# Padding three small tiles so that float32r matmul operands start on multiples of 256 bytes, with a new list of the mixer's steps, in a two-layer decoder trunk

## The chip, the cores and the metric

The kernel runs on one core of one Trainium2 chip. The metric is the device time of one execution in microseconds. A profiled execution has a time of its own and, inside it, a span from the first to the last instruction; the positions in every profile row are counted from the start of that span.

TensorE is called PE in the profile (its weight loads PEld), VectorE DVE, ScalarE ACT, GpSimd POOL, and SyncE, which issues all transfers, SP.

## The reference

A trunk of two layers on 512 tokens of width 1024. Layer 0 mixes tokens with causal average pooling over four windows, layer 1 with stick-breaking attention over 16 heads of 64. Each is followed by a squared-ReLU MLP of width 4096, and both have RMSNorms before and after.

```python
def pool_mixer(h, w_grp, scale):          # four groups of 256 channels, windows 2, 4, 8, 16
    for g, w in enumerate(POOL_WINDOWS):
        outs.append((upper - lower) / count - hf[:, :, sl])      # windowed mean minus identity
    y = jnp.einsum('bsgc,gcd->bsgd', y, w_grp)
    return y * scale

def stick_breaking_attention(q, k, v):    # per block of 128 queries
    z = q_blk @ k_blk.T / 8
    log1m = jnp.where(mask, -jax.nn.softplus(z), 0.0)
    excl = lax.cumsum(log1m, axis=3, reverse=True) - log1m
    a = jnp.where(mask, jnp.exp(jax.nn.log_sigmoid(z) + excl), 0.0)
    return a @ v_blk

def sq_relu_mlp(h, w_up, w_down):
    return jnp.square(jax.nn.relu(h @ w_up)) @ w_down

for layer in range(2):
    h = rms_norm(x, mix_pre_g[layer])
    m = pool_mixer(h, ...) if layer == 0 else stick_breaking_attention(h @ w_q, k, v) @ w_o
    x = x + rms_norm(m, mix_post_g[layer])
    h = rms_norm(x, mlp_pre_g[layer])
    x = x + rms_norm(sq_relu_mlp(h, w_up[layer], w_down[layer]), mlp_post_g[layer])
    if layer == 0:
        k, v = split(rms_norm(x, kv_norm_g) @ w_kv)
```

## The kernel before

**Three products for one.** Nearly every matmul is float32r, a 4-byte format that keeps fewer bits than float32. To keep the precision, an operand is split into a high part (a cast on ACT, L246 or L132) and a low part (the difference on DVE, L247 or L134), and a product becomes three matmuls: high by high, high by low, low by high. The helpers are `mm3` (L267 to L269), `up_block` (L607 to L609) and `Seven.product` (L497). Each matmul loads a stationary operand of 128 columns and streams a moving operand of up to 512.

**The stages.** The tokens are four tiles of 128 rows, x0 to x3.

1. The mixer (layer 0's pooling) from the start to some 49 us. It multiplies each tile by a band matrix (L708), then by the group weights (L731), normalizes, transposes (L765) and splits the result into `xnh` and `xnl`, the high and low parts of the normalized, transposed residual stream, eight slices of 512 tokens each.
2. The first MLP. `up_block` makes one of 32 blocks of 128 hidden channels: 8 slices, three matmuls each, with an up weight stationary and `xnh` or `xnl` moving. The down projection takes 28 of the 32 blocks in five groups by a scheme with seven products in place of eight (class `Seven`; `a` is the stationary operand, `w` the moving one) and the last four plainly through `contract`, with the squares `sq` stationary and the down weights `dn` moving. Blocks of up and products of the group before alternate on PE. The first four up blocks of each MLP are run in two halves of 256 tokens.
3. Attention. Values come from `mm3` with `xnh` or `xnl` stationary and 256 columns moving; keys and queries from `up_block`. Scores are L915 and L916 (q stationary, k or its low part kl moving), the running product is a scan on DVE (L929), the weights are transposed (L947), and L957 multiplies them (ah, al moving) with the values (v stationary). The output projection goes through `contract` with `ohl` stationary and the output weights moving; the last two of its eight weights stand in the tiles that held `v` and `w` (named w and h, l in the profile).
4. The second MLP, as the first. The kernel ends with the last update's norm and stores.

**What sets the order.** Past the mixer the order comes from a scheduler that knows the program order and each instruction's estimated cost, with hints (`issue_after`, `manual_schedule`). In the mixer the order on PE, ACT, DVE and POOL is that of the list `MIX_ORDER` (L42): each word is a step, a letter and its arguments, and each engine runs its steps in the order of the list. The letters used below, with tile t and half h: `q` squares of x (ACT, L679), `r` the power -1/2 (POOL, L690), `b` the band matrix scaled (DVE, L698), `P` pooling (PE, L708), `c` its copy from PSUM to `yt` (ACT, L723 or L719), `L` group weights scaled, four pieces for each of two weight tiles (DVE, L667), `M` group weights (PE, L731), `s` squares of the mixed result (ACT, L250), `g` its gain (DVE, L739), `e` and `E` their total and power, `A` the residual added (DVE, L749), `w` and `v` squares and power for the next norm, `N` that norm (DVE, L756), `T`, `H`, `X` transposes, high and low part (L765, L773, L777), `h`, `l` high and low part of one of the first four up weights (L785, L789), `U` the first half of an up block (PE, L607 to L609). "Tile" 4 stands for the 90 border rows at the seams between tiles, which are loaded into `edge` on their own. A weight's `h` also issues its load on SP (L782) into one of two `raw` buffers, and the third and fourth loads wait until an `l` has freed one.

**Where tiles lie.** A pool lays its tiles one behind another in each partition of SBUF, in steps of 32 bytes. The pool `keep` begins at byte 384: four x tiles of 4104 bytes (4128 with padding), `ident` (512), `gc` (96), `mhalf` (4, takes 32), then `xnh` and `xnl` (16384 each) and the small `stat` tiles; the pools `work` and `wts` follow, and then one pool for the current stage. In the attention pool two tiles `u0` and `u1` of 5124 bytes lie ahead of `v`, `k`, `q`, `w`, `ah`, `al` and `ohl`.

Of the kernel before, what the change touches and what calls it, by code (L numbers as in the profile page):

```python
# [10 lines left out]
F32 = mybir.dt.float32  # L11
# [4 lines left out]
P = 128  # L16
D = 1024
S = 512
T = S // P
KC = D // P  # L20
# [10 lines left out]
EPS = 1e-6  # L31
# [5 lines left out]
NSEG = 1280  # L37
# [3 lines left out]

MIX_ORDER = [  # L42
    (w[0], [int(c) for c in w[1:]])
    for w in """z8 S0 q0 C0 S1 r0 b0 z1 P00 L00 L02 C1 c00 P01 L03 q4 L01 L13 r4 L10 L11 c01 L12 M00 M01 b4 q1 r1 b1 s00
    q2 s01 g00 e0 r2 P40 c40 g01 E0 b2 A0 P10 q3 c10 P11 r3 w0 P20 b3 v0 c11 M10 N00 P30 N01 h0 M11 T00 P31
    l0 s10 h1 c30 g10 s11 l1 c20 e1 g11 H00 E1 A1 X00 c31 h2 T01 M30 M31 w1 v1 l2 s30 N10 s31 M20 H01 N11 T10
    g31 P21 X01 H10 T11 c21 H11 M21 s21 X10 X11 e3 s20 g30 E3 U0 A3 w3 g21 e2 g20 h3 E2 A2 w2 v3 U1 N30 N31
    v2 l3 N21 T30 H30 U2 T21 T31 H31 N20 H21 T20 X30 X31 H20 X21 X20 U3""".split()
]


# [18 lines left out]
def trunk(ctx, tc, x, consts, gcol, grow, pw, wup, wdn, wq, wk, wv, wo, out):  # L70
    nc = tc.nc
    pool = lambda name, bufs=1, **kw: ctx.enter_context(tc.tile_pool(name=name, bufs=bufs, **kw))
    keep = pool("keep")
# [9 lines left out]
    def name(s):  # L83
        uid[0] += 1
        return f"{s}{uid[0]}"
# [4 lines left out]

    xt = [keep.tile([P, D + 2], F32, tag=f"x{t}", name=f"x{t}") for t in range(T)]
    ident = keep.tile([P, P], F32, tag="ident", name="ident")
    gc = keep.tile([P, 3 * KC], F32, tag="gc", name="gc")
    for n in NS:
        nc.sync.dma_start(xt[0][:, n], x[TS[0], n])
    mhalf = keep.tile([P, 1], F32, tag="mhalf", name="mhalf")
# [308 lines left out]
    class Seven:  # L405
# [32 lines left out]
        def squares(self):  # L438
            self.r = self.mp.tile([P, 2, MOST, S], F32, tag="r", bufs=2, name=name("r"))
# [172 lines left out]
    with tc.tile_pool(name="mix0", bufs=1, reuse_waits="tile") as mp:  # L612
# [7 lines left out]
        edge = mp.tile([3 * EDGE, D + 2], F32, tag="edge", name="edge")  # L620
        windows = {**dict(enumerate(xt)), T: edge}
        for w in windows.values():
            nc.vector.memset(w[:, D:], (EPS * D) ** 0.5)

        BANDS = (P, REST, BORDER)
        starts = [0, 4 * P, 4 * (P + REST)]
# [22 lines left out]
        sts, band, pys, pms, ms, xns, pts, pus = {}, {}, {}, {}, {}, {}, {}, {}  # L649
# [27 lines left out]
        def mean_square(t, col):  # L677
            r = rows(t)
            nc.scalar.activation(  # L679
                junk[r, : D + 1], windows[t][:, : D + 1], ACT.Square, scale=D**-0.5,  # L680
                accum_out=sts[t][r, col : col + 1],
            )

        def squares(t):
            sts[t] = keep.tile([P, 8], F32, tag=f"stat{t}", bufs=4, name=name("stat"))
            mean_square(t, 0)

        def power(t, col):
# [102 lines left out]
        def half_up(j):  # L791
            pus[j] = ps(), get(("up", 0, j))
            up_block(*pus[j], slice(0, S // 2))

        steps = {
            "q": squares, "r": lambda t: power(t, 0), "b": scaled_band, "P": pooled, "c": pooled_out,
            "S": spread, "C": spread_out, "L": linear, "M": mixed, "s": mixed_square, "g": mixed_gain,
            "e": total, "E": lambda t: power(t, 4), "A": added, "w": lambda t: mean_square(t, 6),
# [14 lines left out]
    with tc.tile_pool(name="att", bufs=1, reuse_waits="tile") as ap:  # L813
# [75 lines left out]

        begin = ap.tile([P, NSEG], mybir.dt.bfloat16, tag="begin", name="begin")  # L890
        nc.gpsimd.memset(begin, 0.0)
        us = [ap.tile([P, NSEG + 1], F32, tag=f"u{a}", name=f"u{a}") for a in range(2)]
        for lo, n in SEG.values():
            c = min(n - P, 1)
            d = begin[:, lo + n - P - c : lo + n]
# [178 lines left out]
```

## Time and profile before

| What | Value |
|---|---|
| median of 3 runs | 972.52 us (972.29 to 977.75) |
| the profiled execution: its time | 971.85 us |
| its span | 970.0 us |
| granted TensorE clock over the span | 0.997 |
| busy PE, PEld | 951.6 us, 801.0 us |
| busy DVE, ACT, POOL | 709.8 us, 568.7 us, 144.2 us |
| read from and written to HBM | 122.68 MB, 33.55 MB |

A group's row gives line, engine, operation, tiles and shapes, the count, then busy time and mean duration of one in ns, then the engine's idle time just before it and what ended that. A matmul's duration runs from its start to the modelled arrival of its last result, so that durations of successive matmuls overlap: 512 columns take 390 to 395 ns each, though the next one starts sooner. How fast PE goes is read from the distance between starts. A timeline row gives the start, the duration, engine, line, operation and count of a run of like instructions, and in brackets the idle time before it with the releaser. A row of windows gives a stretch of the span, its length, and each engine's busy time with the count of instructions that reach into it.

### The profile page before, as it was taken

How to read it: one execution, taken by the hardware profiler on the slowest of the kernel's cores; microseconds unless marked ns; L12 is line 12 of the kernel's file. 1: busy time of each engine (PE TensorE's matmuls, PEld its weight loads, DVE VectorE, ACT ScalarE, POOL GpSimd, SP SyncE). 2: the span in 40 equal slices, each digit the busy share in tenths (PEclk: the TensorE clock that was granted, in tenths of full speed). 3: DMA queues.
4: the chain of work that ended last, by engine and by line, in shares of the span. 5: the costliest groups of instructions: out<-in, count | busy, mean ns of one | idle time of the engine just before them, and what ended most of it. 6: DMA issues, size and time to landing. Idle time of an engine off the chain costs nothing.

```text
span 970.0 us, 12402 instructions
## 1 busy us (share of the span) xinstructions
PE 951.6 (98%) x4761; PEld 801.0 (83%) x4761; DVE 709.8 (73%) x736; ACT 568.7 (59%) x974; POOL 144.2 (15%) x108
## 2 busy tenths in 40 slices
PE   8999999999999999999999999989999999999997
PEld 6998888888888889888788887888888888888885
DVE  4856797988969966576477787855596876857856
ACT  6657889788865636455655563555544444443632
POOL 2120310502204014000000000301130300403103
PEclk9999999999999999999999999999999999999999
DMA  7544879697696840521624243332503233132012
GB/s 260 187 140 147 309 265 372 228 330 278 232 333 262 304 151 2 217 88 44 244 104 174 88 153 109 131 111 85 191 26 134 105 123 117 44 130 109 29 37 87
DMA packets 43683, 157.03 MB, mean 162 GB/s; under 512 B 4494, under 2 KB 4878, under 8 KB 43625
## 3 DMA queue, kind: packets, MB, share of 16 engines
q1 hardware_dynamic: 43625, 156.25, 45.0%
q8 instruction: 37, 0.61, 0.2%
q14 instruction: 21, 0.17, 0.1%
HBM read 122.68 MB, written 33.55 MB: 161 GB/s over the span
## 4 chain that ended last, share of the span: by engine, by line
PE 92%; DVE 3%; ACT 2%; issue 1%; DMA 1%; SPq 0%; POOL 0%; DVEq 0%; POOLq 0%; ACTq 0%
PE ps L497 28%; PE ps L609 15%; PE ps L607 15%; PE ps L608 15%; PE ps L268 4%; PE ps L269 4%; PE ps L267 4%; PE ps L957 2%; PE ps L947 1%; PE ps L731 1%; DVE e L929 1%; PE ps L915 1%; PE ps L916 1%; DMA edge<-in_x 1%; PE ps L708 1%
## 5 line engine op out<-in xcount | busy, mean ns | idle before, releaser
L497 PE MATMUL ps<-w,a 128*128 128x512 f32 x1176 | 278.8, 390 | 0.0
L608 PE MATMUL ps<-xnl,w 128*128 128x512 f32 (+1 forms) x712 | 265.0, 372 | 0.1
L609 PE MATMUL ps<-xnh,w 128*128 128x512 f32 (+1 forms) x712 | 265.1, 373 | 0.0
L607 PE MATMUL ps<-xnh,w 128*128 128x512 f32 (+1 forms) x712 | 265.0, 373 | 0.0
L497 PEld LDWEIGHTS ps<-w,a 128*128 128x128 f32 x1176 | 220.9, 188 | 47.4
L608 PEld LDWEIGHTS ps<-xnl,w 128*128 128x128 f32 x712 | 134.3, 189 | 25.2 <-DVE xnl L247 0.3
L609 PEld LDWEIGHTS ps<-xnh,w 128*128 128x128 f32 x712 | 134.1, 188 | 25.4
L607 PEld LDWEIGHTS ps<-xnh,w 128*128 128x128 f32 x712 | 134.0, 189 | 24.4
L134 DVE TENSOR_TENSOR w<-raw,w 128x1024 fp32r<-128x1024 f32 x62 | 82.2, 1328 | 62.7 <-ACT w L132 62.7
L132 ACT CAST w<-raw 128x1024 fp32r<-128x1024 f32 x62 | 65.0, 1049 | 87.8 <-PE ps L609 83.4
L506 DVE TENSOR_TENSOR y<-ps,y 128x512 f32<-128x512 f32 x124 | 83.4, 684 | 39.7 <-PE ps L497 39.7
L246 ACT CAST a<-r 128x768 fp32r<-128x768 f32 (+1 forms) x60 | 47.5, 792 | 70.5 <-PE ps L497 46.8
L452 POOL TENSOR_TENSOR s<-r 128x768 f32<-128x768 f32 (+1 forms) x10 | 20.5, 2048 | 382.0 <-ACT r L530 382.0
L247 DVE TENSOR_TENSOR a<-r,a 128x768 fp32r<-128x768 f32 (+1 forms) x60 | 60.1, 1004 | 18.5 <-ACT a L246 18.4
L246 ACT CAST w<-e 128x1536 fp32r<-128x1536 f32 (+1 forms) x30 | 42.0, 1398 | 44.5 <-DVE e L471 33.2
L292 POOL TENSOR_TENSOR y<-y,grow 128x512 f32<-128x512 f32 x12 | 18.7, 1556 | 316.4 <-ACT xn L250 316.4
L452 POOL TENSOR_TENSOR r<-r 128x768 f32<-128x768 f32 (+1 forms) x20 | 52.2, 2608 | 59.3 <-DVE a L247 58.5
L247 DVE TENSOR_TENSOR w<-e,w 128x1536 fp32r<-128x1536 f32 (+1 forms) x30 | 55.9, 1862 | 3.1 <-ACT w L246 2.7
L929 DVE TENSOR_TENSOR_SCAN e<-u,begin 128x1280 f32<-128x1280 f32 x16 | 45.1, 2822 | 13.3 <-ACT u L923 13.0
L143 ACT ACTIVATE apart<-apart,gc 128x128 f32<-128x128 f32 (+1 forms) x132 | 43.0, 405 | 0.0
L250 ACT ACTIVATE xn<-y 128x512 f32<-128x512 f32 (+1 forms) x25 | 15.4, 615 | 41.8 <-DVE y L359 41.8
L247 DVE TENSOR_TENSOR w<-xn,w 128x1536 fp32r<-128x1536 f32 (+1 forms) x20 | 33.0, 1651 | 6.4 <-ACT w L246 6.4
(137 smaller groups left out, 1486.5 us busy)
## 6 DMA issues: line engine op xcount, KB each, us to landing
raw<-in_wup SPq DMA_DIRECT2D x62, 512.0 KB, 4.1
w<-kept SPq DMA_DIRECT2D x58, 512.0 KB, 4.1
kept<-wx SPq DMA_DIRECT2D x30, 512.0 KB, 4.3
w<-in_wdn SPq DMA_DIRECT2D x8, 1536.0 KB, 6.7
kept<-apart SPq DMA_DIRECT2D x24, 512.0 KB, 3.6
xn<-in_wdn SPq DMA_DIRECT2D x8, 1536.0 KB, 8.0
raw<-in_wdn SPq DMA_DIRECT2D x8, 512.0 KB, 3.7
apart<-in_wk SPq DMA_DIRECT2D x7, 512.0 KB, 6.5
```

The lines of the kernel that those rows point to most:

```text
L132: nc.scalar.copy(hi, raw)
L134: nc.vector.tensor_tensor(out=lo, in0=raw, in1=hi.bitcast(F32), op=ALU.subtract)
L143: nc.scalar.mul(c, c, gc[:, lo + k : lo + k + 1])
L246: latest["act"] = nc.scalar.copy(hi, src)
L247: latest["dve"] = nc.vector.tensor_tensor(out=lo, in0=src, in1=hi.bitcast(F32), op=ALU.subtract)
L452: sub = lambda out, x, y, op=ALU.subtract: nc.gpsimd.tensor_tensor(out=out, in0=x, in1=y, op=op)
L497: nc.tensor.matmul(bank, a[:, x, q, TS[t]], w[:, z, q], start=start and q == 0 and k == 0, stop=q == self.n - 1 and k == 2, skip_group_che ...
L506: nc.vector.tensor_tensor(out=part, in0=bank, in1=part, op=ALU.add)
L607: nc.tensor.matmul(pu[:, cols], wh[:, k, :], xnh[:, k, cols], start=k == 0, stop=False)
L608: nc.tensor.matmul(pu[:, cols], wh[:, k, :], xnl[:, k, cols], start=False, stop=False)
L609: nc.tensor.matmul(pu[:, cols], wl[:, k, :], xnh[:, k, cols], start=False, stop=k == KC - 1)
L929: nc.vector.tensor_tensor_scan(out=e[:, ::-1], data0=u[:, 1:][:, ::-1], data1=begin[:, ::-1], initial=0.0, op0=ALU.mult, op1=ALU.max,)
```

## The change

Four edits change where tiles lie. `gc` gets 32 more elements (128 bytes) of which nothing is used; the `stat` tile of the border rows has 16 elements instead of 8; `u1` gets 55 more elements, unused. The two extra columns of the x tiles are now addressed as two, which is what they were. The list of the mixer's steps is another one; it has the same steps.

```diff
-    for w in """z8 S0 q0 C0 S1 r0 b0 z1 P00 L00 L02 C1 c00 P01 L03 q4 L01 L13 r4 L10 L11 c01 L12 M00 M01 b4 q1 r1 b1 s00
...
+    for w in """z8 q0 S0 r0 C0 b0 S1 z1 P00 L01 C1 L02 L00 P01 L03 L12 c00 c01 M00 q4 L10 r4 L11 s00 L13 b4 q1 r1 M01 s01
...
-    gc = keep.tile([P, 3 * KC], F32, tag="gc", name="gc")
+    gc = keep.tile([P, 3 * KC + 32], F32, tag="gc", name="gc")[:, : 3 * KC]
...
-            nc.vector.memset(w[:, D:], (EPS * D) ** 0.5)
+            nc.vector.memset(w[:, D : D + 2], (EPS * D) ** 0.5)
...
-            sts[t] = keep.tile([P, 8], F32, tag=f"stat{t}", bufs=4, name=name("stat"))
+            sts[t] = keep.tile([P, 16 if t == T else 8], F32, tag=f"stat{t}", bufs=4, name=name("stat"))
...
-        us = [ap.tile([P, NSEG + 1], F32, tag=f"u{a}", name=f"u{a}") for a in range(2)]
+        us = [ap.tile([P, NSEG + 1 + 55 * a], F32, tag=f"u{a}", name=f"u{a}")[:, : NSEG + 1] for a in range(2)]
```

In the two built programs the operands of the float32r matmuls begin so many bytes past a multiple of 256 (the count is that of matmuls in the program):

| Matmuls | count | moving operand, before -> after | stationary operand, before -> after |
|---|---|---|---|
| up and projections, 512 columns (L607 to L609) | 1704 | 128 -> 0 | 0 -> 0 |
| up and projections, 256 columns (L607 to L609) | 432 | 128 -> 0 | 0 -> 0 |
| values (L267 to L269, 256 columns) | 384 | 0 -> 0 | 128 -> 0 |
| output projection (L267 to L269, ohl) | 192 | 0 or 64 -> 0 | 64 -> 0 |
| scores (L915, L916) | 128 | 64 (k), 0 (kl) -> 0 | 64 -> 0 |
| attention weights by values (L957) | 128 | 64 -> 0 | 64 -> 0 |
| seven products (L497) | 1176 | 0 -> 0 | 0 -> 0 |
| plain down products (L267 to L269, dn and sq) | 204 | 0 -> 0 | 0 -> 0 |

`xnh` begins at byte 17536 before (68 x 256 + 128) and 17664 after (69 x 256); `k` of the first head at 162112 (633 x 256 + 64) and 162560 (635 x 256). The pools behind `keep` begin 256 bytes later.

The new list moves instructions on four engines inside the mixer. On ACT, its steps after the first square of x0 and the first copy of the scale row stood so before (a copy `scale`, then tile 0's pooled halves into `yt`, and the squares of x, of the border rows `edge` and of mixed results into `stat`):

```order
L723 COPY yt<-ps_143 128x4x128
L679 ACTIVATE junk,stat_158<-edge 90x1025
L723 COPY yt<-ps_152 128x4x128
L679 ACTIVATE junk,stat_179<-x_71 128x1025
L250 ACTIVATE junk,stat_134<-ps_167 128x512
L679 ACTIVATE junk,stat_185<-x_72 128x1025
```

and stand so now:

```order
L723 COPY yt<-ps_143 128x4x128
L723 COPY yt<-ps_152 128x4x128
L679 ACTIVATE junk,stat_166<-edge 90x1025
L250 ACTIVATE junk,stat_132<-ps_161 128x512
L679 ACTIVATE junk,stat_175<-x_71 128x1025
L250 ACTIVATE junk,stat_132<-ps_178 128x512
L679 ACTIVATE junk,stat_206<-x_72 128x1025
```

The second copy into `yt` (step c01) has moved ahead of the border rows' squares (q4), and the squares of tile 0's first mixed half (s00) ahead of those of x1 (q1).

On PE the same list stands, from tile 0's second mixed half on, before (`pw` are the group weights, `band` the scaled band matrices, `xn` the normalized rows):

```order
L731 MATMUL ps_172<-pw_100,yt 128x256 x4
L708 MATMUL ps_192<-band_177,edge 128x46 x8
L708 MATMUL ps_209<-band_182,x_71 128x114 x4
L708 MATMUL ps_217<-band_182,x_71 128x114 x4
L708 MATMUL ps_224<-band_206,x_72 128x114 x4
L731 MATMUL ps_233<-pw_99,yt 128x256 x4
L708 MATMUL ps_239<-band_229,x_73 128x114 x4
L731 MATMUL ps_249<-pw_100,yt 128x256 x4
```

and now:

```order
L731 MATMUL ps_178<-pw_100,yt 128x256 x4
L708 MATMUL ps_185<-band_173,edge 128x46 x8
L708 MATMUL ps_196<-band_194,x_71 128x114 x4
L708 MATMUL ps_201<-band_194,x_71 128x114 x4
L708 MATMUL ps_223<-band_218,x_72 128x114 x4
L731 MATMUL ps_231<-pw_100,yt 128x256 x4
L731 MATMUL ps_237<-pw_99,yt 128x256 x4
L708 MATMUL ps_245<-band_229,x_73 128x114 x4
```

The first five stand in the same places; of what follows, tile 1's second half is multiplied ahead of the first. Past the mixer each engine has at most a few neighbours exchanged: on SP the second weight load of the first MLP has moved ahead of one of a later key weight.

More of the change, by code (lines that the diff above doesn't have):

```diff
@@ L43 @@
     (w[0], [int(c) for c in w[1:]])
-    for w in """z8 S0 q0 C0 S1 r0 b0 z1 P00 L00 L02 C1 c00 P01 L03 q4 L01 L13 r4 L10 L11 c01 L12 M00 M01 b4 q1 r1 b1 s00
[L45 to L48, printed above, removed]
+    for w in """z8 q0 S0 r0 C0 b0 S1 z1 P00 L01 C1 L02 L00 P01 L03 L12 c00 c01 M00 q4 L10 r4 L11 s00 L13 b4 q1 r1 M01 s01
+    e0 P40 b1 P11 P10 q2 c40 r2 c11 E0 q3 g00 b2 g01 r3 c10 P21 A0 b3 M11 w0 M10 s11 c21 v0 P31 N00 g11 s10
+    T00 P30 h0 M21 e1 c31 g10 E1 c30 N01 A1 P20 H00 T01 w1 X00 h1 v1 l0 s21 N11 M30 T11 c20 N10 T10 H01 M20
+    l1 H11 X11 H10 X10 s30 M31 X01 h2 s20 h3 g21 l2 s31 g20 e2 g30 E2 e3 E3 U0 A2 w2 g31 U1 A3 v2 U2 l3 N20
+    w3 T20 H20 v3 N31 T31 N30 N21 T30 H31 X20 X31 T21 H30 X30 U3 H21 X21""".split()
 ]
```

## The prediction

> **What bounds the kernel now.** I read the page's engine totals and its chain of waits first, then busy time by stage.
>
> ```profile
> PE 951.6 (98%) x4761; PEld 801.0 (83%) x4761; DVE 709.8 (73%) x736; ACT 568.7 (59%) x974; POOL 144.2 (15%) x108
> ...
> PE 92%; DVE 3%; ACT 2%; issue 1%; DMA 1%; SPq 0%; POOL 0%; DVEq 0%; POOLq 0%; ACTq 0%
> ...
> 49.00:366.00 317.00, 317.00 (x1425) 260.71 (x1424) 258.45 (x232) 231.64 (x384) 57.58 (x26) 1.00 0.71 256
> 390.00:630.00 240.00, 236.70 (x1381) 207.66 (x1380) 170.22 (x200) 131.99 (x292) 10.02 (x11) 1.00 0.37 136
> 637.00:900.00 263.00, 263.00 (x1198) 216.77 (x1198) 183.07 (x158) 127.07 (x153) 44.99 (x19) 1.00 0.30 106
> ```
>
> The last three rows are stretches of the span (length, then PE, PEld, DVE, ACT, POOL busy, granted clock, DMA share): the first MLP, attention, the second MLP. PE is 92% of the chain, and in both MLPs it is busy for the whole stretch while the next engine, DVE, works 258.45 of 317.00 and 183.07 of 263.00. So the time is how far apart matmuls start, plus the few waits that the mixer and attention leave. A busy PE hides the first of these; the starts in the timeline show it. First the groups by form, for the counts:
>
> ```profile
> L497 PE MATMUL ps<-w,a 128*128 128x512 f32 x1176 | 278.8, 390 | 0.0
> L609 PE MATMUL ps<-xnh,w 128*128 128x512 f32 x568 | 224.5, 395 | 0.0
> L608 PE MATMUL ps<-xnl,w 128*128 128x512 f32 x568 | 224.2, 395 | 0.0
> ...
> L268 PE MATMUL ps<-w,ohl 128*128 128x512 f32 x56 | 22.4, 399 | 2.2 <-DVE w L134 2.2
> ...
> L267 PE MATMUL ps<-h,ohl 128*128 128x512 f32 x8 | 3.2, 395 | 0.0
> ```
>
> Then a stretch near the end of the second MLP (start, duration; only PE's rows are kept), and two windows asked for PE alone:
>
> ```profile
> 922.95 0.40 PE L607 MATMUL ps<-xnh,w 128*128 128x512 f32 x1
> ...
> 928.54 8.34 PE L497 MATMUL ps<-w,a 128*128 128x512 f32 x36
> 936.72 0.39 PE L267 MATMUL ps<-dn,sq 128*128 128x512 f32 x1
> ...
> 944.88:959.83 14.95, 14.95 (x67) 1.00 0.19 70
> 505.87:517.02 11.15, 11.15 (x50) 1.00 0.26 94
> ```
>
> From 922.95 to 928.54 stand one up block's 24 matmuls (8 slices, L607 to L609): 5.59/24 = **232.9 ns** apart. From 928.54 to 936.72 stand 36 of L497: 8.18/36 = **227.2 ns**. The first window holds 66 of the down projection's plain products (L267 to L269, dn and sq; the 67th reaches in from ahead): 14.95/66 = 226.5 ns. The second holds the 48 of a key and a query projection (two more reach in): 11.15/48 = 232.3 ns. All are 512 columns of float32r behind a 128-column weight load, without a wait, at clock 1.00. By the change's table of addresses the two at 227 have both operands on a multiple of 256 bytes; up and the projections have the moving one (xnh, xnl) 128 bytes past it.
>
> **The change part by part.**
>
> *Up blocks and projections.* 568 triples of 512 columns start 128 bytes off before and 0 after. 448 of them are in the MLPs (28 blocks of 8 in each; the other 4 blocks go in halves), 120 in attention. At L497's 227.2: 1344 x (232.9 - 227.2) = 7.7 us, and 360 x (232.3 - 227.2) = 1.8 us. **Together -9.5 us**, all on the path, since nothing else holds PE in these stretches; the padding adds no instruction. Bounds: 0, if the address isn't the cause; with the best row (226.5) 1344 x 6.4 + 360 x 5.8 = -10.7.
>
> *Output projection and attention products.* Here the stationary operand (ohl) or both (k and q) lie 64 bytes off:
>
> ```profile
> 604.86 0.39 PE L269 MATMUL ps<-h,ohl 128*128 128x512 f32 x1
> ...
> 607.41 0.39 PE L268 MATMUL ps<-l,ohl 128*128 128x512 f32 x1
> ...
> 571.61 0.39 PE L915 MATMUL ps<-k,q 128*128 128x512 f32 x1
> ...
> 572.07 0.33 PE L915 MATMUL ps<-k,q 128*128 128x384 f32 x1
> ```
>
> Eleven starts with ohl from 604.86 to 607.41: 231.8 ns. Against 227.2 that is 4.6 x 192 (3 x 56 and 3 x 8) = -0.9 us. The two 512-wide products from 571.61 to 572.07 are 230 apart; 64 such (16 in each of four groups) save 0.2 us, and as many of 384 columns, for which no aligned row exists, 0 to 0.3. I take **-1.2 us** for all. That a stationary operand's offset shows as well, in the same helper that runs dn and sq at 226.5, is the second pair of rows for the address.
>
> *256 columns.* Up halves (128 bytes off), then dn and sq (both on 256):
>
> ```profile
> 628.31 0.29 PE L608 MATMUL ps<-xnl,w 128*128 128x256 f32 x1
> ...
> 629.50 0.28 PE L609 MATMUL ps<-xnh,w 128*128 128x256 f32 x1
> ...
> 959.95 0.28 PE L268 MATMUL ps<-dn,sq 128*128 128x256 f32 x1
> ...
> 962.59 0.28 PE L269 MATMUL ps<-dn,sq 128*128 128x256 f32 x1
> ```
>
> Ten steps in 1.19 against 22 in 2.64: 119 and 120 ns. Aligned is no faster there, so the value and key halves count nothing.
>
> *The mixer's list.* Its first difference on ACT is that c01, the second half of tile 0's pooled copy, stands ahead of q4, the squares of the border rows.
>
> ```profile
> 10.67 1.27 DVE L667 SCALAR_TENSOR_TENSOR pw<-pw,gc,scale 128x256 f32<-128x256 f32 x3
> 12.37 1.06 ACT L679 ACTIVATE junk<-edge 90x1025 f32<-90x1025 f32 x1 [3.56 <-DMA edge<-in_x]
> 13.42 0.56 ACT L723 COPY yt<-ps 128x512 f32<-128x512 f32 x1
> 13.59 0.55 POOL L690 TENSOR_TENSOR stat<-stat,mhalf 90x1 f32<-90x1 f32 x1 [7.64 <-ACT junk L679]
> 13.89 1.06 ACT L679 ACTIVATE junk<-x 128x1025 f32<-128x1025 f32 x1
> 14.04 1.99 PE L731 MATMUL ps<-pw,yt 128*128 128x256 f32 x8 [2.62 <-ACT yt L723]
> 14.18 0.31 DVE L698 TENSOR_SCALAR band<-bands,stat 90x184 f32<-90x184 f32 x1 [2.24 <-POOL stat L690]
> 15.07 0.60 ACT L250 ACTIVATE junk<-ps 128x512 f32<-128x512 f32 x1
> 15.70 0.46 DVE L698 TENSOR_SCALAR band<-bands,stat 128x456 f32<-128x456 f32 x1 [1.22 <-POOL stat L690]
> 15.79 1.06 ACT L679 ACTIVATE junk<-x 128x1025 f32<-128x1025 f32 x1
> 15.87 1.88 PE L708 MATMUL ps<-band,edge 90*128 90x46 f32 x16
> 17.57 2.91 PE L708 MATMUL ps<-band,x 128*128 128x114 f32 x24
> ...
> 35.41 0.47 PE L607 MATMUL ps<-xnh,w 128*128 128x256 f32 x1
> ```
>
> Before, ACT stands 3.56 us for the border rows' transfer with c01 queued behind, and PE stands 2.62 us for c01. After, c01 runs while ACT would wait; M01 (1.83 us, from 14.04 to 15.87) then needs only the second weight's scaling, which ends at 10.67 + 1.27 = 11.94, and is over by about 13.7. The next late thing is the border band: transfer, squares, power (13.59 to 14.14), band (14.18 to 14.49). P40 can start near 14.55 instead of 15.87. Behind it, P11 waits for band 1: on ACT the square s00 (15.07 to 15.79, so 0.72) now precedes q1, which starts at 13.42 + 0.72 = 14.14 instead of 13.89, so the band ends at 16.16 + 0.25 = 16.4 and P11 starts at 16.5 instead of 17.57: 1.1 earlier. From there PE has the same work. SP's queue keeps its order in the mixer; the weight casts h and l move later on ACT and DVE, and the third and fourth weight loads, which wait for a low part to free their buffer, go with them. They have the two earlier half blocks as cover; if that is gone, U2 or U3 waits. Bounds: -2.6 (PE's whole wait) and +1 (one late square or cast); I take **-1.2 us**, near the worked -1.1.
>
> *Other.* A few swaps of neighbours past the mixer (on DVE and ACT a weight part against a square or low part, on SP two weight loads) leave each engine's total the same: 0. In attention PE waits for DVE's weight parts (the 2.2 us in the row of w and ohl above); with an earlier PE such waits grow. I give back **+0.3 us**, as a share of the 1.8 us gained in projections.
>
> *Sum.* -9.5 - 1.2 - 1.2 + 0.3 = -11.6 us. The profiled execution took 971.85 (span 970.0), so 960.25; the median of the runs is 0.67 above it: **960.9**.
>
> *A rule and a row.* The rows say 232 to 233 with an operand 64 or 128 bytes past a multiple of 256, and 227 on it. The Trainium skill (SBUF — State Buffer, Specifications (TRN2)) gives SBUF 16-byte cachelines. By that rule 64, 128 and 0 all begin a line, the lines read stay as many, and the first two terms would be nothing. This trace disagrees as far as its 5.7 ns go, and it has no row that shows an offset at the aligned step.
>
> **The rivals.**
>
> *The address is not the cause* (0.13). Up also differs from L497 in that 24 matmuls accumulate in one bank, against 9 or 6, and that the activations move and the weights stand still. For it: 256 columns show no gain. Against: products with dn and sq and with ohl come from one helper, the weights move in both, and they are 5 ns apart. Only the mixer's 1.2 us stay: 971.3. This is where the cacheline rule leads.
>
> *Another engine becomes the bound* (0.04). PE in the first MLP goes from 317 to 313 while DVE has 258 to do: 83%. It would take weight parts arriving late block by block. If that eats half of the first term, 965.7.
>
> *Slower: the new relative position costs* (0.04). In the built program all aligned pairs of before lie 256 bytes past a multiple of 512, both operands alike. After it, xnh and xnl lie 256 past 512 and up's weights on it, a pair that no row shows. Should reading them together take the longer of the steps now seen in up, as from 924.34 to 924.58 below, 240 instead of 232.9, 1704 matmuls add 12.1 us; less 2.1 for the other two terms: 982.5. The deciding point is 2.1 us/1704 = 1.2 ns above today's step; from 6.9 ns above it (11.8 us) the kernel is over 1% slower.
>
> ```profile
> 924.34 0.40 PE L607 MATMUL ps<-xnh,w 128*128 128x512 f32 x1
> 924.58 0.39 PE L608 MATMUL ps<-xnl,w 128*128 128x512 f32 x1
> ...
> 629.62 1.04 PE L324 MATMUL ps<-ident,xn 128*128 128x128 f32 x8
> 634.00 1.94 PE L324 MATMUL ps<-ident,xn 128*128 128x128 f32 x8 [3.35 <-DVE xn L315]
> ```
>
> The last two rows are what blurs the forecast itself: after a wait of 3.35 us at the end of attention the same eight transposes take 1.94 instead of 1.04, at a lower granted clock. Whether that comes again may shift the time by 1.5 us either way (0.9 here and some for the first half block).
>
> **How the numbers follow.** My forecast has 0.79; its own range is 957.5 to 964: the sum with its best rows (-1.2 for up, -1.4 for the mixer, -1.5 for the clock, not all at once) and its worst (+2.2 mixer, +1.5 clock). The rivals have 0.13, 0.04 and 0.04. From 957 to 967 the range holds the forecast and the second rival, about 0.82. About 1%, 9.7 us, is what a measurement of this kernel tells from no change: 962.8 is that border, 1.9 above my forecast, and a late clock or a poorer mixer takes 0.08 of the 0.79 across it: faster 0.71. Within 1% get that 0.08, the first rival's 0.13 and the second's 0.04: 0.25. Slower 0.04.
>
> **What would show it.** Right: 24 up matmuls in 5.45 us instead of 5.59, L497 unchanged at 227 ns; 48 of a projection in 10.9; PE's 2.62 us wait before L731 gone and one of about 1 us before the border's L708; the first up matmul near 34.2 instead of 35.41; DVE's waits on PE shorter. Wrong: up still near 233 ns (first rival), L497 or up above it (third), or PE waiting for DVE inside the MLPs (second).

## The result, and the profile after

The changed kernel took 964.70 us (median of 5 runs, 962.68 to 967.47) beside 972.52 of the kernel before: a ratio of 0.991, with a 95% interval of 0.988 to 0.994. In two later comparisons, each on one chip, it took 961.93 beside 972.31 and 963.24 beside 972.67, ratios 0.989 [0.986, 0.992] and 0.990 [0.986, 0.994]. The forecast was 960.9, with a range of 957 to 967. So the sign and the range held, and the gain was 7.8 to 10.4 us instead of 11.6. The forecast had given 0.71 to a gain of more than 1% (a time below 962.8); of the three medians only 961.93 is such a gain.

The profiled execution took 967.47 us (span 965.7, granted clock 0.991), the slowest of the five; it is called the first profile below. Its groups by form (columns as before):

```profile
L497 PE MATMUL ps<-w,a 128*128 128x512 f32 x1176 | 278.2, 390 | 1.2 <-DVE a L247 1.2
L607 PE MATMUL ps<-xnh,w 128*128 128x512 f32 x568 | 221.4, 390 | 0.0
L608 PE MATMUL ps<-xnl,w 128*128 128x512 f32 x568 | 221.4, 390 | 0.0
L609 PE MATMUL ps<-xnh,w 128*128 128x512 f32 x568 | 221.3, 390 | 0.0
```

Up and projections now take 390 ns each, as L497 does; they took 395. In the timeline of PE near the end of the second MLP, a block of up (24 matmuls) and 36 of L497; then a key and a query projection in attention (48 matmuls from the first row to the last):

```profile
918.79 0.39 PE L607 MATMUL ps<-xnh,w 128*128 128x512 f32 x1
...
924.23 8.32 PE L497 MATMUL ps<-w,a 128*128 128x512 f32 x36
932.39 0.39 PE L267 MATMUL ps<-dn,sq 128*128 128x512 f32 x1
```

```profile
505.38 0.40 PE L607 MATMUL ps<-xnh,w 128*128 128x512 f32 x1
...
516.29 2.35 PE L947 MATMUL ps<-ident,w 128*128 128x128 f32 x20
```

(924.23 - 918.79)/24 = 226.7 ns, where it was 232.9; L497 (932.39 - 924.23)/36 = 226.7, where it was 227.2; the projections 10.91/48 = 227.3, where they were 232.3. The first term of the sum is there.

The mixer looks otherwise. Rows of ACT and PE in its first part, the first matmul of up, and two windows (the last three figures are granted clock, DMA share, GB/s):

```profile
10.80 3.84 PE L731 MATMUL ps<-pw,yt 128*128 128x256 f32 x16 [0.90 <-ACT yt L723]
...
13.26 1.06 ACT L679 ACTIVATE junk<-edge 90x1025 f32<-90x1025 f32 x1 [2.74 <-DMA edge<-in_x]
...
15.44 1.98 PE L708 MATMUL ps<-band,edge 90*128 90x46 f32 x16 [0.80 <-DVE band L698]
...
38.14 0.47 PE L607 MATMUL ps<-xnh,w 128*128 128x256 f32 x1
```

```profile
15.00:20.00 5.00, 4.29 (x27) 4.17 (x28) 2.55 (x6) 3.79 (x12) 1.67 (x4) 0.73 1.02 411
20.00:25.00 5.00, 5.00 (x22) 4.70 (x22) 2.49 (x3) 2.96 (x6) 1.09 (x2) 0.58 0.09 35
```

PE's wait of 2.62 us for the second copy is gone, and one of 0.80 us for the border's band has come, near the 1 us that was worked out. But the border rows landed 0.89 us later (13.26, was 12.37), and the granted clock fell to 0.73 and 0.58: half speed for 6.8 us. Up begins at 38.14 instead of 35.41, not at 34.2.

And PE now waits inside the first MLP, where it did not: 1.2 us in three pieces for `a` (the row of L497 above). DVE and POOL in the group in which the longest of them arises:

```profile
232.66 1.76 DVE L471 TENSOR_TENSOR e<-xn,w 128x1536 f32<-128x1536 f32 x1 [2.16 <-DMA xn<-in_wdn]
...
236.37 2.57 POOL L452 TENSOR_TENSOR s<-r 128x768 f32<-128x768 f32 x1 [42.41 <-ACT r L530]
...
237.15 3.41 DVE L471 TENSOR_TENSOR w<-w 128x1536 f32<-128x1536 f32 x1
...
239.02 3.25 POOL L452 TENSOR_TENSOR r<-r 128x768 f32<-128x768 f32 x1
```

DVE waits 2.16 us for the second down weights (0.57 before). Its L471 on `w` then begins after POOL's L452 and takes 3.41 us; before, it began at 234.76, ahead of POOL's first at 235.72, and took 1.75. From there DVE works without a break up to the left operands (L247, `a`), and these come late for PE, which waits for them until 251.59.

### The profile page after: what moved, and what is told of

Read it like the earlier page. It is cut to its first block, busy times and chain, and to the rows that moved or that the text cites. A ratio compares the mean times of both kernels' runs of the same rounds, so it can differ in the third digit from the quotient of the medians.

```text
span 965.7 us, 12404 instructions
## 1 busy us (share of the span) xinstructions
PE 947.1 (98%) x4761; PEld 806.2 (83%) x4761; DVE 711.1 (74%) x736; ACT 566.9 (59%) x974; POOL 142.1 (15%) x108
## 4 chain that ended last, share of the span: by engine, by line
PE 73%; DVE 11%; DMA 5%; issue 5%; ACT 5%; POOL 0%; POOLq 0%; DVEq 0%; SPq 0%; ACTq 0%
PE ps L497 18%; PE ps L608 11%; PE ps L607 11%; PE ps L609 11%; PE ps L268 4%; PE ps L269 4%; PE ps L267 4%; DMA xn<-in_wdn 3%; DVE w L247 2%; DMA raw<-in_wup 2%; PE ps L957 2%; PE ps L947 2%; DVE w L134 2%; DVE e L471 2%; PE ps L731 1%
## 5 line engine op out<-in xcount | busy, mean ns | idle before, releaser
L497 PE MATMUL ps<-w,a 128*128 128x512 f32 x1176 | 278.2, 390 | 1.2 <-DVE a L247 1.2
L608 PE MATMUL ps<-xnl,w 128*128 128x512 f32 (+1 forms) x712 | 262.8, 369 | 0.1
L609 PE MATMUL ps<-xnh,w 128*128 128x512 f32 (+1 forms) x712 | 262.5, 369 | 0.0
L607 PE MATMUL ps<-xnh,w 128*128 128x512 f32 (+1 forms) x712 | 262.4, 370 | 0.0
L497 PEld LDWEIGHTS ps<-w,a 128*128 128x128 f32 x1176 | 220.6, 188 | 48.0 <-DVE a L247 2.4
L609 PEld LDWEIGHTS ps<-xnh,w 128*128 128x128 f32 x712 | 135.0, 190 | 22.2
L608 PEld LDWEIGHTS ps<-xnl,w 128*128 128x128 f32 x712 | 135.0, 190 | 22.0 <-DVE xnl L247 0.3
L607 PEld LDWEIGHTS ps<-xnh,w 128*128 128x128 f32 x712 | 134.7, 190 | 21.8
L134 DVE TENSOR_TENSOR w<-raw,w 128x1024 fp32r<-128x1024 f32 x62 | 82.3, 1327 | 65.3 <-ACT w L132 65.2
L452 POOL TENSOR_TENSOR s<-r 128x768 f32<-128x768 f32 (+1 forms) x10 | 21.4, 2144 | 371.3 <-ACT r L530 352.7
L247 DVE TENSOR_TENSOR a<-r,a 128x768 fp32r<-128x768 f32 (+1 forms) x60 | 60.0, 1002 | 16.5 <-ACT a L246 16.4
L247 DVE TENSOR_TENSOR w<-e,w 128x1536 fp32r<-128x1536 f32 (+1 forms) x30 | 59.6, 1988 | 3.1 <-ACT w L246 2.7
L452 POOL TENSOR_TENSOR r<-r 128x768 f32<-128x768 f32 (+1 forms) x20 | 50.5, 2523 | 66.1 <-DVE a L247 65.3
L529 ACT ACTIVATE r<-ps 128x512 f32<-128x512 f32 x56 | 33.0, 590 | 6.8 <-PE ps L609 6.8
```

Source lines behind the costliest of these rows:

```text
L134: nc.vector.tensor_tensor(out=lo, in0=raw, in1=hi.bitcast(F32), op=ALU.subtract)
L247: latest["dve"] = nc.vector.tensor_tensor(out=lo, in0=src, in1=hi.bitcast(F32), op=ALU.subtract)
L452: sub = lambda out, x, y, op=ALU.subtract: nc.gpsimd.tensor_tensor(out=out, in0=x, in1=y, op=op)
L497: nc.tensor.matmul(bank, a[:, x, q, TS[t]], w[:, z, q], start=start and q == 0 and k == 0, stop=q == self.n - 1 and k == 2, skip_group_che ...
L607: nc.tensor.matmul(pu[:, cols], wh[:, k, :], xnh[:, k, cols], start=k == 0, stop=False)
L608: nc.tensor.matmul(pu[:, cols], wh[:, k, :], xnl[:, k, cols], start=False, stop=False)
```

## The experiments

**The change in its parts.** Four kernels on one chip, with the kernel before at 972.31 (15 runs).

```diff
 # e1: the four edits on tiles, the list of before
 # e2: the new list, the tiles of before
 # e3: both (the changed kernel itself)
 # e4: the list of before, and of the tiles only these, which move xnh and xnl
+    gc = keep.tile([P, 3 * KC + 32], F32, tag="gc", name="gc")[:, : 3 * KC]
+            sts[t] = keep.tile([P, 16 if t == T else 8], F32, tag=f"stat{t}", bufs=4, name=name("stat"))
```

> The three pads without the new list of mixer steps. Theory (the padding brings all of the gain, and the new list trips the granted clock in the mixer and loses some 3 us there): up matmuls 227 ns apart as with both edits, no stretch at half clock between 15 and 25 us, first whole up block some 3 us earlier than in the profile of both edits, time 960.5 to 962.5 us. Rival (the half clock in the mixer came by chance or from the late first loads, the list itself brings its 1.2 us): time 1 us above that of both edits, 964 to 966 us. Open in both: whether PE waits three times some 0.6 us for DVE at the ends of groups of the first MLP, as with both edits; if it does here too, the list isn't the cause of these.

> The new list of mixer steps without the pads. Theory: a stretch of 3.4 us or more at half clock after the border rows' pooling, the first whole up block 1 to 3 us later than before, no PE wait for DVE inside the first MLP, up matmuls 233 ns apart, time 973 to 975.5 us. Rival (the list brings its 1.2 us): 971.3 us.

> The changed kernel once more, beside its parts on the same chip. Theory: 963 to 966 us, with the half clock in the mixer's first third again, and three waits of PE for DVE in the first MLP. Rival (chance): 960 to 962 us, without the stretch at half clock.

> The old list, and of the pads only the two ahead of xnh and xnl: attention's operands stay 64 bytes off. Theory of the forecast's second term (1.2 us for output projection, scores and values): 1 to 1.3 us above the run with all pads, output projection 232 ns apart, up 227. Rival (attention hides it under its waits): the same time as with all pads.

| Kernel | median, us | ratio, 95% interval |
|---|---|---|
| e1, tiles only | 964.03 | 0.992 [0.989, 0.995] |
| e2, list only | 971.88 | 0.999 [0.998, 1.001] |
| e3, both | 961.93 | 0.989 [0.986, 0.992] |
| e4, xnh and xnl only | 964.48 | 0.992 [0.989, 0.995] |

The padding brings 8 us, and the place of xnh and xnl nearly all of it (e4). The list alone brings nothing that can be measured, and on top of the padding 2.1 us, with intervals that overlap. If attention's operands were worth 1.2 us, e4 was to stand 1 to 1.3 above e1; it stands 0.4 above, less than the runs of either kernel differ, so these times do not size that term.

Rows of the mixer with the list alone (e2), as those of the changed kernel above:

```profile
9.62 3.67 PE L731 MATMUL ps<-pw,yt 128*128 128x256 f32 x16
...
11.69 1.06 ACT L679 ACTIVATE junk<-edge 90x1025 f32<-90x1025 f32 x1 [1.28 <-DMA edge<-in_x]
...
13.87 1.98 PE L708 MATMUL ps<-band,edge 90*128 90x46 f32 x16 [0.58 <-DVE band L698]
...
16.12 2.93 PE L708 MATMUL ps<-band,x 128*128 128x114 f32 x24 [0.28 <-DVE band L698]
...
33.49 0.47 PE L607 MATMUL ps<-xnh,w 128*128 128x256 f32 x1
```

The mixer's start hangs on when the border rows land, which differs from execution to execution (10.95 to 13.52 us over the thirteen profiles of this study). From their squares to the first matmul of up it is 33.49 - 11.69 = 21.80 us here. In e3 it is 21.80 too (11.13 to 32.93), and in the kernel before 35.41 - 12.37 = 23.04; e1 and e4 have 23.01. **So the list is worth 1.2 us in the mixer**, as forecast, and the half speed there in the first profile is not its doing: e2 and e3 have the list without it, and one of the runs below has it with the old list.

Why nothing was left of that in e2's profile shows later, in the output projection's second group. Rows of DVE and PE in e3 (the list alone has the same some 5 us later), then two windows of e3 around it, one of the list alone, and one of the kernel before:

```profile
570.83 2.83 DVE L929 TENSOR_TENSOR_SCAN e<-u,begin 128x1280 f32<-128x1280 f32 x1
...
573.79 1.49 DVE L933 TENSOR_TENSOR w<-w,e 128x1280 f32<-128x1280 f32 x1
...
575.20 1.22 DVE L134 TENSOR_TENSOR w<-raw,w 128x1024 fp32r<-128x1024 f32 x1
...
576.47 0.50 PE L268 MATMUL ps<-w,ohl 128*128 128x512 f32 x1 [1.97 <-DVE w L134]
```

```profile
575.00:580.00 5.00, 3.53 (x12) 2.92 (x13) 4.57 (x8) 0.18 (x1) 0.00 (x0) 0.75 0.30 105
580.00:585.00 5.00, 5.00 (x33) 4.52 (x32) 4.50 (x9) 4.19 (x9) 0.00 (x0) 0.91 0.41 114
```

```profile
580.00:585.00 5.00, 3.12 (x8) 2.44 (x9) 4.11 (x7) 0.00 (x0) 0.00 (x0) 0.70 0.31 105
```

```profile
580.00:585.00 5.00, 3.05 (x14) 2.33 (x14) 4.71 (x7) 0.33 (x2) 0.00 (x0) 1.00 0.38 125
```

PE waits 2 us for a weight's low part, which DVE makes only behind a scan and a product. The kernel before waits as long there (the last row, busy 3.05 of 5.00), and its clock stays at 1.00. In these profiles of the list alone and of the change the clock drops behind the wait, and 1.3 to 1.6 us are lost: with the list alone PE is 1.7 us ahead of the kernel before up to there, and 0.1 from there on.

Neither the list nor the padding decides this. In each of the thirteen traces the granted clock changes only at whole multiples of 3.413 us from its first rise to full speed (in e3 that is at 4.02 us, and 577.46 = 4.02 + 168 x 3.413). Two such stretches of e3, then two of the kernel before:

```profile
574.05:577.46 3.41, 1.44 (x7) 0.99 (x6) 3.25 (x5) 0.00 (x0) 0.00 (x0) 1.00 0.02 7
577.46:580.87 3.41, 3.41 (x14) 2.93 (x13) 2.90 (x5) 0.76 (x2) 0.00 (x0) 0.50 0.43 154
...
578.84:582.25 3.41, 2.77 (x15) 2.18 (x13) 3.28 (x2) 1.49 (x3) 0.00 (x0) 1.00 0.72 286
582.25:585.66 3.41, 2.10 (x10) 1.74 (x10) 3.25 (x7) 0.00 (x0) 0.00 (x0) 1.00 0.31 78
```

In e3 the whole wait lies in one stretch, of which PE is busy for 0.42, and the next stretch runs at half speed. In the kernel before a boundary cuts the wait, PE is busy for 0.81 and 0.62 of the two stretches, and the clock stays. So it is in all thirteen: the seven profiles with half speed near 577 (the first one, e1, e2, e3, s4, v0, v1) have PE busy for 0.42 to 0.43 of the stretch ahead of it, and the other six (before, e4, s1, s2, s3, v2) for at least 0.49 of every stretch there. Where the stretches fall differs from execution to execution.

**Which start counts.** Four kernels with the list and the gaps of before, in which xnh, xnl or the weights begin elsewhere; elements are added behind them so that all later tiles stay on their multiples.

```diff
 # s1, s2: xnh and xnl 32 and 64 bytes past a multiple of 256 (n = 40, 48)
+    gc = keep.tile([P, 3 * KC + n], F32, tag="gc", name="gc")[:, : 3 * KC]
...
 # s3: xnh on it (n = 32), xnl 128 past it
+    xnh = keep.tile([P, KC * S + 32], F32R, tag="xnh", name="xnh")[:, : KC * S].rearrange("p (k s) -> p k s", k=KC)
...
 # s4: both on it, the weights of up, projections and output projection 128 past it
+        raw = wts.tile([P, D + 16], F32, tag="raw", bufs=2, name=name("raw"))[:, :D]
...
```

> The old list and the old gaps, but xnh and xnl begin 32 bytes past a multiple of 256 (before: 128); 64 bytes behind them keep all later buffers where they were. Theory (any start off a multiple of 256 costs the same extra piece of every row read): the up blocks step by 232 to 234 ns on average, alternating 229 and 237 as before, L497 stays at 227, and the time is that of before, 971 to 973. Rival A (the cost grows with the distance from the multiple, 32 being a quarter of 128): 228 to 229 ns and about 965. Rival B (a coarser or a finer grid decides, 32 or 64 bytes): with a grid of 32 bytes, 227 ns and 964.

> As the run with 32 bytes, with xnh and xnl 64 bytes past a multiple of 256. Theory: 232 to 234 ns, 971 to 973. Rival A: 229 to 230 ns, about 967. Rival B, a grid of 64 bytes: 227 ns here and 233 in the run with 32 bytes.

> xnh begins on a multiple of 256, xnl 128 bytes past one; all else as before. Two of an up block's three products read xnh, one xnl. Theory (each matmul pays for its own operand): the steps in a triple differ, two at 227 and one at 233 to 239, a mean of 229 to 231, and a third to two thirds of the gain: 966 to 969. Rival (what counts is that both activations lie alike, or one misplaced operand sets the pace of the whole group): all steps at 233, 972. Second rival (only xnh, read twice, counts): 227, 964.

> xnh and xnl begin on a multiple of 256, as in the changed kernel, and the weight pairs of up, projections, values and output projection begin 128 bytes past one, where they began on it; in up and the projections that is the stationary operand, 128 columns. Theory (a stationary operand's start counts as a moving one's does, as the step of the output projection with ohl 64 bytes off suggested): up steps by 230 to 233 ns, and the time is 968 to 973. Rival (the stationary operand's load runs beside the matmul and its start costs nothing): 227 ns and 964, and the old gap at the output projection came from something else.

One run each, beside 971.37 for the kernel before on that chip. Executions of one kernel differ by up to some 5 us (v0 below: 961.75 to 966.77), so the steps carry what follows, and the times less. The groups of up and projections by form, for s1, s2, s3 and s4 in turn (in s4 a line is added, so that L608 to L610 stand for L607 to L609):

```profile
L607 PE MATMUL ps<-xnh,w 128*128 128x512 f32 x568 | 225.0, 396 | 0.0
L609 PE MATMUL ps<-xnh,w 128*128 128x512 f32 x568 | 224.7, 396 | 0.0
L608 PE MATMUL ps<-xnl,w 128*128 128x512 f32 x568 | 224.4, 395 | 0.0
```

```profile
L607 PE MATMUL ps<-xnh,w 128*128 128x512 f32 x568 | 223.9, 394 | 0.0
L609 PE MATMUL ps<-xnh,w 128*128 128x512 f32 x568 | 223.0, 393 | 0.0
L608 PE MATMUL ps<-xnl,w 128*128 128x512 f32 x568 | 221.9, 391 | 0.0
```

```profile
L608 PE MATMUL ps<-xnl,w 128*128 128x512 f32 x568 | 224.3, 395 | 0.0
L607 PE MATMUL ps<-xnh,w 128*128 128x512 f32 x568 | 222.0, 391 | 0.0
L609 PE MATMUL ps<-xnh,w 128*128 128x512 f32 x568 | 221.5, 390 | 0.0
```

```profile
L608 PE MATMUL ps<-xnh,w 128*128 128x512 f32 x568 | 224.7, 396 | 0.0
L610 PE MATMUL ps<-xnh,w 128*128 128x512 f32 x568 | 224.3, 395 | 0.0
L609 PE MATMUL ps<-xnl,w 128*128 128x512 f32 x568 | 224.1, 395 | 0.0
```

| Kernel | moving, stationary: bytes past a multiple of 256 | mean step of up and projections, ns | L497, ns | time, us |
|---|---|---|---|---|
| before | 128, 0 | 233.0 | 227.5 | 971.37 |
| s1 | 32, 0 | 233.5 | 228.5 | 973.69 |
| s2 | 64, 0 | 229.7 | 229.1 | 968.60 |
| s3 | xnh 0, xnl 128; 0 | 228.1, 233.3, 227.3 (L607, L608, L609) | 226.9 | 965.42 |
| s4 | 0, 128 | 232.9 | 227.6 | 974.29 |
| e4 | 0, 0 | 227.0 | 227.0 | 964.48 (another chip) |

The steps are distances from start to start, all of a kind in one profile; those of before are from the first chip's profile of it. In s3 the matmul with the displaced operand is slow and its two neighbours hardly are: **each matmul pays in the main for its own operands.** In s4 the moving operands lie right and the weights do not, and it is as slow as before: **the stationary operand's start counts as much**. The theory that any displacement costs the same holds for 32 and 128 bytes and not for 64, which costs half as much; a cost that grows with the distance is ruled out by 32 bytes. Displacements also slow L497, which lies on multiples throughout: 229.1 in s2, 226.9 where at least xnh lies right. The slow ones stand just behind an up block: before, the first three take 231.2, 232.8 and 230.4 ns on average and those from the fourth on 227; in s1 the first seven are touched, in s2 the first ten.

The times fit the steps, with what the mixer and the clock add. For s1: 1704 x 0.5 and 1176 x 1.0 ns give +2.0 (measured +2.3). For s2: 1704 x -3.3 and 1176 x 1.6 give -3.7, and 1.5 us of half speed in the mixer, with the old list, make it -2.2 (measured -2.8). For s3: 1704 x -3.4 and 1176 x -0.6 give -6.5 (measured -6.0). s4 has 1.4 us of half speed near 577 us, and its border rows landed 1.15 later than in the first chip's profile of before: +2.4 (measured +2.9). With one run each, agreement to 0.6 us is partly luck.

The Trainium skill (SBUF — State Buffer, Specifications (TRN2)) gives SBUF 16-byte cachelines. Starts at 32, 64 and 128 bytes all begin such a line and cost 6.5, 2.7 and 6 ns against 0 here, so its lines do not tell what a start costs.

**The wait of 2 us.** The changed kernel once more (v0); a kernel in which the output projection's weight chunks 2 and 3 are split ahead in the first MLP like the others (v1); and that with 20 transposes of the identity where PE waits for the last tile's norm at the end of attention (v2).

```diff
 # v1
-            apart.extend(x for x in queue[n:] if x[0] not in [("o", c) for c in range(4)])
+            apart.extend(x for x in queue[n:] if x[0] not in [("o", c) for c in range(2)])
...
-        steps = [n for n in range(1, 34)] if l == 0 else []
+        steps = [n for n in range(34)] if l == 0 else []
...
+        if l == 0:
+            with tc.issue_after(latest["act"].ins), tc.issue_after(latest["dve"].ins):
+                split_apart(mp)
 # v2, besides: ahead of the last tile's transposes in the second MLP
+                    for _ in range(busy):
+                        nc.tensor.transpose(pt[:, TS[0]], ident, ident)
...
```

> The changed kernel itself, unaltered, as the base for the two runs beside it: 961 to 965, a wait of PE of about 2.0 us for a weight's low part (L134) near 577 us of the span, half clock behind it for about 3.4 us, and a wait of about 3.3 us near 627 with half clock behind it.

> The changed kernel, with the output projection's weight chunks 2 and 3 split into high and low part in the first MLP, as the others already are, instead of in attention (32 weights split ahead instead of 30: one more call ahead of the first step and one more step). Nothing is left out. Theory (the list's and the pads' gain is given back at the output projection's second group: PE waits 2.0 us for L134, which DVE does only after two scans and products, and half clock follows for 3.4 us, which costs 1.3 to 1.6): both go, and the time is 3.0 to 3.6 us below the changed kernel's on this chip, some 958 to 961. Rival A (DVE's later work in that stretch, the transposes' products of the next heads, ends last then): the wait moves and 0 to 1 us is gained. Rival B (half clock comes there whatever PE waits for): 2.0 is gained and the half clock stays. Rival C (two more weights in the first MLP, 3 MB more of DMA there, lengthen its waits for DVE's operands): up to 1.5 us is lost there.

> As the run with chunks 2 and 3 split ahead, and 20 transposes of the identity (0.13 us each, 2.6 us) on PE at the end of attention, where it waits 3.3 us for the last tile's norm; they write a bank that the real transposes then overwrite. Nothing is left out. Theory (half clock follows from idling, so work of no use keeps the clock): eight transposes take 1.03 instead of 1.56 to 1.94 us and the first half blocks step by 119 instead of 213 ns: 1.2 to 1.8 us less than without them. Rival (the clock drops there for another reason, or a stretch of idling of 0.7 us is enough): the half clock stays, and the time is the same or up to 0.3 us longer.

| Kernel | median, us (4 runs) | ratio to before on that chip (972.67) |
|---|---|---|
| v0, changed | 963.24 (961.75 to 966.77) | 0.990 [0.986, 0.994] |
| v1 | 963.33 (961.71 to 963.94) | 0.989 [0.985, 0.993] |
| v2 | 962.39 (960.01 to 964.87) | 0.988 [0.984, 0.992] |

v1 went as its rival A said: the wait for L134 is gone, and a few matmuls further on another of the same length has come, with half speed behind it. A row of DVE and one of PE in v1 (L835 and L960 are L832 and L957 of the kernel before):

```profile
577.90 0.42 DVE L835 TENSOR_TENSOR v<-ps,v 128x256 fp32r<-128x256 f32 x1
...
578.37 0.33 PE L960 MATMUL ps<-ah,v 128*128 128x128 f32 x1 [2.10 <-DVE v L835]
```

The low part of the last heads' values stands on DVE behind the same scan and product that held back L134. Undoing one of two late steps gained nothing: 963.33 beside 963.24.

In v2, the end of attention (L324 with `ident` alone are the added transposes, L327 the real ones, L615 the first up matmul), and for comparison the last tile's transposes in e3:

```profile
624.76 2.35 PE L324 MATMUL ps<-ident 128*128 128x128 f32 x20
...
628.13 1.38 PE L327 MATMUL ps<-ident,xn 128*128 128x128 f32 x8 [1.02 <-DVE xn L315]
629.27 0.36 PE L615 MATMUL ps<-xnh,w 128*128 128x256 f32 x1
```

```profile
627.77 1.56 PE L324 MATMUL ps<-ident,xn 128*128 128x128 f32 x8 [3.28 <-DVE xn L315]
```

With work in the gap the clock stays up in v2's profile: from 625 to 640 us the granted clock is 1.00 there, and 0.77 to 0.89 in all twelve other profiles. In those twelve one stretch of 3.413 us there has PE busy for 0.06 to 0.37; in v2 the emptiest has 0.67. Over this stretch v2 gains 1.3 us on v1 in the two profiles. The medians differ by 0.9, within what these runs scatter, so v2 is likely the best of the kernels here, but not shown to be.

## Why the prediction was right, and where it was not

*Up blocks and projections, -9.5.* Right, in mechanism and size. The distances between their starts, waits left out, sum to 397.0 us before, 387.3 in the first profile and with the tiles alone (e1), and 387.1 in e3: 9.7 to 9.9 less. The first rival, the address not being the cause, fell with e4 and with s3, where one operand of two is displaced and only its matmul is slow. The third, that a pair in the new relative position costs, fell too: xnh and xnl now lie 256 past a multiple of 512, the weights on one, and the step is 227.

*Output projection and attention products, -1.2.* The 0.9 for `ohl` were there: the median step with `ohl` went from 233 to 227 ns. Not every such matmul was slow, though: the eight of L269 with h and ohl stood at 228 on average before as after, so the profile of before did hold a row with an offset near the aligned step. The 0.2 to 0.3 for scores and values were not: their 512-column steps stand at 231 to 235 ns with both operands on multiples, as before. The step of the working that failed is that they, too, would fall to L497's step. They stand alone or in pairs between products of other widths, never in a train of 512 columns. That would fit L497, whose first matmul behind an aligned up block takes 231.7 ns in e4 and the next 227; whether it is the reason was not tried.

*256 columns, 0.* Nearly right: the starts of L607 to L609 with 256 columns took 52.67 us before and 53.83 with the tiles alone (e1), +1.2, most of it at half speed. At full speed the aligned step is 119.9 ns where it was 118.9: alignment costs some 1 ns here, 0.4 us in 432 matmuls.

*The mixer's list, -1.2.* Right in size: 23.04 became 21.80 in four profiles (e2, e3, v0, v1). The path was in part another. Counted from the border rows' squares, their pooling starts 1.32 us earlier (2.18 behind them in e2, 3.50 before), as worked out, but tile 1's (P11) only 0.76 earlier (4.44, was 5.20) and not 1.1, for PE waits 0.28 us for its band. The other 0.5 came further on, where the working had PE do the same work; that the sum came out is luck to that extent. The bounds of -2.6 to +1 took in the working, but nothing in the sum or its range spoke of half speed in the mixer, which cost 3.1 us in the first profile (24.88 from the border's squares to up, against 21.80), 1.6 in v2 and, with the old list, 1.5 in s2.

*Given back in attention, +0.3.* Mis-sized. The clock blur was named for the end of attention alone. The wait for the low part near 577 us was in the row quoted (2.2 us), but not that half speed may follow it, as it does in seven of the thirteen profiles, where it costs 1.3 to 1.6 us.

*Another engine becomes the bound* had 0.04 and came true in small: waits of PE on DVE in the first MLP, none before, come with the padding (for `a`, in us: e1 0.4, e3 0.7, the first profile 1.2, e4 1.4, v0 2.2) and not with the list alone. The reason given against it, DVE at 258 of 317 us, is an average over the stage; the waits come some 60 us apart, once in a group (189.76, 251.59 and 311.15 in the first profile), where DVE is busy without a break. In v0 half speed followed one of them. Its row of PE's waits (total, times, longest), and two of its windows:

```profile
PE ps L497 <- DVE a L247: 2.2, 2, 1.4
```

```profile
300.00:310.00 10.00, 8.14 (x33) 6.03 (x32) 10.00 (x9) 0.84 (x1) 2.03 (x1) 0.94 0.60 192
310.00:320.00 10.00, 10.00 (x41) 8.14 (x40) 9.93 (x9) 7.82 (x9) 3.46 (x1) 0.88 0.71 256
```

v0 was 3.9 us ahead of the kernel before at the 450th matmul of L497, and 0.5 at the 588th, the last of this MLP.

*The sum.* Against the changed kernel's best profile, e3, 10.3 us in span: -9.9 in up and projections, -0.7 in L497, -1.2 list, -1.2 because the border rows landed earlier in that execution, -0.9 `ohl`, +1.3 half speed near 577 and +0.7 waits in the first MLP make -11.9; the 1.6 that are left are about what the 256-column groups took more (1.2 in up, 0.2 in the values). So the gains were right to within 1 us, and the 3.8 us by which 964.7 lies over the forecast fit waits that were there before or are new, with the half speed that some executions add. The first five runs bear this out in part: they took 962.68 us at a mean granted clock of 0.995, 964.50 to 964.97 at 0.993 and 967.47 at 0.991, and one more stretch of 3.413 us at half speed lowers that mean by 0.002. So some 2 of the 3.8 us go with the clock; how the other 1.8 divide stays open. The two later medians lie 1.0 and 2.3 over the forecast.

## What to carry to other kernels

When equal matmuls step by different amounts without a wait, compare where their operands start, the stationary ones too, and look for rows that differ in that alone; here it was worth 6 ns in 233, and a few unused elements ahead of a buffer set it right. Add to a sum of gains on a busy engine the waits near which it works already: with 2 us of idling the next 3.4 us may run at half speed, in one execution and not in the next, by where its clock's stretches fall. A wait removed from an engine whose supplier is busy behind it without a break moves to that supplier's next product.

## What the runs showed of the hardware

- A float32r matmul of 512 columns behind a weight load steps by 227 ns with both operands on multiples of 256 bytes; 32 or 128 bytes past it by 233, 64 bytes past it by 230. Either operand is enough (the stationary one was tried at 128). With 256 columns the order is the reverse and the differences small: 119.9 ns on multiples, 118.9 at 128 bytes, 117.8 at 64, 116.9 at 32.
- The slow steps are not uniform: before, they were mostly 229 or 237 to 238; in s2 L607, L608 and L609 had 231.5, 228.0 and 229.7 on average, and before, the eight of L269 with h and ohl had 228 though ohl lies 64 bytes off. And displaced matmuls slow the first three to ten aligned ones behind them (L497 up to 229.1 over the whole program).
- The clock changed at multiples of 3.413 us in every profile, and until the last stores half speed lasted one such stretch, twice two (the mixer of the first profile, the end of attention in s1). From the MLPs and attention at full speed it followed stretches of which PE was busy for 0.06 to 0.37 (the end of attention), 0.42 to 0.43 (near 577, seven profiles) or 0.46 (v0, behind waits of 0.5 and 1.4 us close together), and none of 0.49 or more. In the mixer, where matmuls have 46 to 256 columns, the busy share does not tell: half speed followed 0.36 (s2), 0.77 (the first profile) and 0.82 (v2), and not 0.46 (before). The Trainium skill (TensorE: Matmul & The Clock Gate, What's actually happening) tells of a window of 3413 ns that runs on its own and does not start with the kernel; the multiples and the lengths agree with that. Its table there has the low clock after at least one idle window of about 3.4 us, and its section Why this matters for your kernels warns of gaps above some 3 us; here 2 us were enough where they fell into one stretch, and less at times.
- DVE's L471 takes up to 3.41 us instead of 1.75 where POOL's L452 had begun before it and was still running. Where L471 began first, it took 1.75 though L452 started while it ran (before, at 172.93, 234.76 and 296.64). The Trainium skill (SBUF — State Buffer, Who interferes with whom) says that a DVE instruction with two SBUF inputs contends with a GpSimd instruction that reads SBUF; these rows agree.
